# Low parts of two weight blocks in the Strassen pair jobs: a negated copy and an adding transfer in place of a VectorE subtraction

## The chip, the cores and the metric

The kernel runs on one core of one Trainium2 chip. The metric is the device time of one execution in microseconds, the median of several runs. The core has a matrix engine (PE; its weight loads are shown apart as PEld), VectorE (DVE), ScalarE (ACT), GpSimd (POOL), SyncE (SP, which here only issues transfers) and 16 DMA engines that all queues share.

## The reference

One layer of a streaming encoder, 512 tokens of width 1024, all in float32: a first SwiGLU feed-forward network (FFN) with half-step residual, a mixer (a gated recurrent branch and a windowed attention branch), and a second FFN of the same form. Each sub-layer stands between two RMS norms.

```python
def swiglu(x, w1, w3, w2):
    return (jax.nn.silu(x @ w1) * (x @ w3)) @ w2

f = swiglu(rms_norm(h, ffn1_pre_g[l]), ffn1_w1[l], ffn1_w3[l], ffn1_w2[l])   # D_FF = 2816
h = h + 0.5 * rms_norm(f, ffn1_post_g[l])
...
h = h + rms_norm(merged @ w_o[l], mix_post_g[l])
f = swiglu(rms_norm(h, ffn2_pre_g[l]), ffn2_w1[l], ffn2_w3[l], ffn2_w2[l])
return h + 0.5 * rms_norm(f, ffn2_post_g[l])
```

## The kernel before

**Numbers in two parts.** The matrix engine takes a rounded 32-bit type (`float32r`). To keep float32 accuracy every operand is held as a high part (the value rounded, written by an ACT copy) and a low part (the value minus its high part, written by a DVE subtraction). `split2` (lines 193 to 196) does the two. Every product is three: high weights by high data, low weights by high data, high weights by low data (lines 205 to 207, or 845 to 847 in the pair jobs).

**The stages.** The head loads x, transposed, and the first three weight units in quarters (lines 1000 to 1008): `load_x` brings one row block of x, `load_w(u, kp)` a quarter of weight unit u. All go out on SP's queue but the first block of x, which ACT issues. While these land, nine products on zeros warm the matrix engine (line 998); after that lines 1034 to 1048 split each quarter and multiply it. Then come the first units of FFN 1, its pair jobs, its second product (w2), the mixer, the first units of FFN 2, its pair jobs, and its w2 with the final norm.

**The pair jobs** (class `Pairs`, lines 850 to 972). The two hidden products of an FFN, x @ w1 and x @ w3, are done for two blocks of 128 hidden columns at a time, as a 2 x 2 block product with Strassen's seven products in Winograd's form. A job is one weight matrix for one pair of blocks; jobs alternate between w1 and w3. FFN 1 has 16 jobs, FFN 2 has 18. The two weight tiles `ra` and `rb` (512 KB each, 128 partitions of 4 KB) hold the blocks a11, a12 and a21, a22, 512 columns each. `prep(m, i)` prepares job m in five pieces, most of them while job m - 1 runs:

- i = 0: four block sums by DVE into the tiles S12 and S34 (lines 888 to 891).
- i = 1: high and low part of a11 and a12 together, that is of the whole tile `ra` (line 893, through `both` and `split2`).
- i = 2 and i = 3: the same for S12 and S34.
- i = 4: the same for a22; then the raw tiles and the sums are given back.

`run` (lines 904 to 972) writes a job's order by hand. Each `mm_s` is one of the seven products, 12 matmuls of 128 x 128 by 256 columns: a11 into bank bu, ACT copies bu to q1; s1 into bank bx, ACT copies bx to q5; then the previous job's last product, a22 (`last`, lines 961 to 970); then `prep(n + 1, 1)`; s2, added into bu, and ACT copies it to u; `prep(n + 1, 2)`; a12 (`c11`); s4 and DVE's sum; `prep(n + 1, 3)`; s3 and DVE's sum; Silu by ACT after a w1 job or the product of the two halves by DVE after a w3 job; `prep(n + 1, 4)`, `prep(n + 2, 0)` and the loads for job n + 3 by SP.

Within each engine this is the order of execution: nothing reorders it. Engines wait for each other by semaphores at the tiles. The first product of job n + 1 reads the high part of a11 in its first matmul and the low part in its second. In job 0 of FFN 1 there are also `late` hooks (lines 1179 to 1183): high and low parts of the data blocks b22, t3 and t4, which are first read in that job and the next.

**What sets the order around it.** Before the pair jobs, work is queued with `later(n, fn)` and run at `point()`, which `mm_feat` and `mm_s` call; the five pieces of job 0 are placed by hand (lines 1064 to 1068 and 1084 for FFN 1, 1550 for FFN 2). All tiles of 4 KB a partition come from one pool of 43 slots, in which a tile that is written waits for the last reader of the tile before it.

Of the kernel before, what the change touches and what calls it, by code (L numbers as in the profile page):

```python
# [11 lines left out]
F32R = mybir.dt.float32r  # L12
AF = mybir.ActivationFunctionType
ALU = mybir.AluOpType

P = 128
# [35 lines left out]
def hybrid_layer(ctx: ExitStack, tc: tile.TileContext, a: dict, out: bass.AP):  # L52
    nc = tc.nc
    act, dve, pool, pe, sp = nc.scalar, nc.vector, nc.gpsimd, nc.tensor, nc.sync
# [8 lines left out]
    def slot(shape, dt=F32, name="s"):  # L63
        uid[0] += 1
        return sb.tile(shape, dt, tag="slot", name=f"{name}_{uid[0]}")

    def bank(name="ps"):
        uid[0] += 1
        return pp.tile([P, 512], F32, tag="ps", name=f"{name}_{uid[0]}")
# [95 lines left out]
    def get(nm, i, ahead=2, rawahead=3):  # L165

        k = st["get"]
        assert order[k] == (nm, i), (order[k], nm, i)
        dma_to(k + 1 + ahead)
        split_to(k + 1 + ahead)  # L170
        dma_to(st["split"] + rawahead)
        st["get"] += 1
        return pairs.pop(k)
# [5 lines left out]
    def later(n, fn, rank=1):  # L179
        uid[0] += 1  # L180
        due.append((now[0] + n, rank, uid[0], fn))
# [11 lines left out]
    def split2(hi, lo, src):  # L193

        act.activation(hi, src, AF.Copy)  # L195
        dve.tensor_tensor(out=lo, in0=src, in1=f32(hi), op=ALU.subtract)  # L196
# [14 lines left out]
    def unit(nm, i, **kw):  # L211
        w = get(nm, i)
        ps = bank("f")
        mm_feat(ps, w, **kw)
        return ps
# [273 lines left out]
    def w2_gemm(nm, hid, gpost_name, scale, gpre_name, first, h_src, h_dst):  # L489
# [159 lines left out]
        for due_, cost, fn, k in reversed(plan):  # L649
            cur = min(cur, due_ - W2_LEAD) - cost / W2_FILL  # L650
            if fn:
# [184 lines left out]
    QH = 4 * P  # L836
# [13 lines left out]
    class Pairs:  # L850
# [13 lines left out]
        def prep(self, m, i):  # L864
            if m >= len(self.jobs):
                return
            k = self.k0 + 2 * m
            if i == 0:
                if k not in loaded or k + 1 not in loaded:
                    self.raws(m)  # L870
                s12, s34 = slot([P, 2 * QH], name="S12"), slot([P, 2 * QH], name="S34")
                self.w[m] = {"r": (raws.pop(k), raws.pop(k + 1)), "s": (s12, s34)}
            W = self.w[m]
            (ra, rb), (s12, s34) = W["r"], W["s"]
            a11, a12, a21, a22 = ra[:, :QH], ra[:, QH:], rb[:, :QH], rb[:, QH:]

            def both(src, w=2 * QH):
                hi = slot([P, w], F32R, name="whi")
                lo = slot([P, w], F32R, name="wlo")
                split2(hi, lo, src)  # L880
                return hi, lo

            def halves(p, a, b):
                W[a] = p[0][:, :QH], p[1][:, :QH]
                W[b] = p[0][:, QH:], p[1][:, QH:]

            if i == 0:
                dve.tensor_tensor(out=s12[:, :QH], in0=a21, in1=a22, op=ALU.add)
                dve.tensor_tensor(out=s12[:, QH:], in0=s12[:, :QH], in1=a11, op=ALU.subtract)
                dve.tensor_tensor(out=s34[:, QH:], in0=a12, in1=s12[:, QH:], op=ALU.subtract)  # L890
                dve.tensor_tensor(out=s34[:, :QH], in0=a11, in1=a21, op=ALU.subtract)
            elif i == 1:
                halves(both(ra), "a11", "a12")
            elif i == 2:
                halves(both(s12), "s1", "s2")
            elif i == 3:
                halves(both(s34), "s3", "s4")
            elif i == 4:
                t = slot([P, 2, QH], F32R, name="w22")
                split2(t[:, 0, :], t[:, 1, :], a22)  # L900
                W["a22"] = t[:, 0, :], t[:, 1, :]
                del W["r"], W["s"]

        def run(self, tail, hooks={}):
            X = self.X
            assert st["get"] == st["split"] == self.k0, (st, self.k0)
            st["get"] = st["split"] = self.k0 + 2 * len(self.jobs)
            last = lambda: None
            for n, (nm, f) in enumerate(self.jobs):
                W = self.w.pop(n)  # L910
                first = nm == self.na
                tmp = slot([P, 4, 256], name="ct")
                q1, q5, u = (tmp[:, i, :] for i in range(3))
                c = slot([P, 2, SEQ], name="cc")
                if first:
                    self.c1[f] = c
                bu, bx, bc = (bank("c")[:, :256] for _ in range(3))
                at = lambda i: [f() for f in hooks.get((n, i), ())]
                mm_s(W["a11"], X["b11"], bu)
                act.activation(q1, bu, AF.Copy)  # L920
                if n == len(self.jobs) - 1:
                    tail()
                at(1)
                mm_s(W["s1"], X["t1"], bx)
                act.activation(q5, bx, AF.Copy)
                at(2)
                last()
                self.prep(n + 1, 1)
                mm_s(W["s2"], X["t2"], bu, True)
                del W["s1"], W["s2"]  # L930
                act.activation(u, bu, AF.Copy)
                at(3)
                self.prep(n + 1, 2)

                def c11():
                    mm_s(W["a12"], X["b21"], bc)
                    del W["a11"], W["a12"]
                    dve.tensor_tensor(out=c[:, 0, :256], in0=bc, in1=q1, op=ALU.add)

                if n < len(self.jobs) - 1:  # L940
                    c11()
                mm_s(W["s4"], X["b22"], bx, True)
                dve.tensor_tensor(out=c[:, 0, 256:], in0=bx, in1=u, op=ALU.add)
                self.prep(n + 1, 3)
                mm_s(W["s3"], X["t3"], bu, True)
                del W["s3"], W["s4"]
                dve.tensor_tensor(out=c[:, 1, 256:], in0=bu, in1=q5, op=ALU.add)
                if n == len(self.jobs) - 1:
                    c11()
                if first:  # L950
                    act.activation(c[:, 0, :], c[:, 0, :], AF.Silu)
                    act.activation(c[:, 1, 256:], c[:, 1, 256:], AF.Silu)
                else:
                    c1 = self.c1[f]
                    dve.tensor_tensor(out=c1[:, 0, :], in0=c1[:, 0, :], in1=c[:, 0, :], op=ALU.mult)
                    dve.tensor_tensor(out=c1[:, 1, 256:], in0=c1[:, 1, 256:], in1=c[:, 1, 256:], op=ALU.mult)
                self.prep(n + 1, 4)
                self.prep(n + 2, 0)
                self.raws(n + 3)

                def last(W=W, bu=bu, c=c, f=f, first=first):
                    mm_s(W.pop("a22"), X["t4"], bu, True)
                    if first:
                        act.activation(c[:, 1, :256], bu, AF.Silu)
                    else:
                        c1 = self.c1.pop(f)
                        dve.tensor_tensor(out=c1[:, 1, :256], in0=bu, in1=c1[:, 1, :256], op=ALU.mult)
                        if f in self.hid.apart:
                            self.hid.c[f] = c1
                        self.hid.f += [c1[:, 0, :], c1[:, 1, :]]  # L970

            last()
# [7 lines left out]
    raw3 = [slot([P, D], name="raw_first") for _ in range(NS)]  # L980
# [4 lines left out]
    def load_x(k, q=sp):  # L985
        q.dma_start(out=xts[k // 2][:, k % 2, :], in_=a["xT"][k * P : (k + 1) * P, :])

    def load_w(u, kp):
        nm, i = order[u]
        c = slice(kp * 2 * P, (kp + 1) * 2 * P)  # L990
        sp.dma_start(out=raw3[u][:, c], in_=a[nm][i * P : (i + 1) * P, c])


    warm = slot([P, 512], F32R, name="warm")
# [3 lines left out]
        pe.matmul(psw, warm[:, :P], warm, start=True, stop=True)  # L998

    load_x(0, act)  # L1000
    sp.dma_start(out=vec, in_=a["vec"])
    for kp in range(KT // 2):
        load_w(0, kp)
        if kp:
            load_x(2 * kp)
        load_w(1, kp)
        load_w(2, kp)
        load_x(2 * kp + 1)
    dma_to(NS + 2)
# [5 lines left out]
    pairs_a = Pairs("w1a", "w3a", NC1, X1, hid)  # L1015
# [48 lines left out]
    pairs_a.prep(0, 0)  # L1064
    ps.append(unit("w3a", 1))
    pairs_a.prep(0, 1)
    p1 = unit("w1a", 2)
    pairs_a.prep(0, 2)

# [103 lines left out]
    end = 2 * 2 * (NC1 - 2)  # L1173
# [163 lines left out]
    for t in range(NT):  # L1337
        ps = bank("v")
        c = slice(t * P, (t + 1) * P)
# [207 lines left out]
        later(2 + i, lambda i=i: X2.update({f"t{i + 1}": to_slots(tn[i])}))  # L1547
    pairs_b = Pairs("w1b", "w3b", NC2, X2, hid)
    end = 2 * 2 * (NC2 - 2)
    for i, at_ in enumerate((end - 7, end - 4, end - 3, end - 2, end - 1)):  # L1550
        later(at_, lambda i=i: pairs_b.prep(0, i))
    later(end, lambda: pairs_b.prep(1, 0))
    swiglu_units("w1b", "w3b", 2, NC2, hid)
# [23 lines left out]
PRE_AT = {"xr": [("w2b", 2, 2, 2), ("w2b", 8, 8, 2)], "xg": [("w2b", 4, 7, 1)], ("wg", 13): [("w2b", 6, 1, 1)], "wao": [("w2b", 14, 4, 1)]}  # L1577
W2_LOAD = (14, 9, 8, 8)
P0A, P0B = 6, 8
W2_LEAD = 2.5  # L1580
W2_RAW = 4
W2_FLUSH = 2.5
# [57 lines left out]
```

## Time and profile before

| | us |
|---|---|
| median of 3 runs | 1120.33 (1120.18 to 1120.45) |
| profiled execution | 1120.09 |
| its span, first instruction to last | 1118.3 |
| PE busy | 1109.7 |
| PEld busy | 987.7 |
| DVE busy | 907.3 |
| ACT busy | 607.8 |
| POOL busy | 34.7 |

The span is the time from the first to the last instruction that the profile shows; the rest of an execution's time lies around it. The pair jobs run from 72.4 to 235 us (FFN 1) and from 820.5 to 1003 us (FFN 2). In a row of the timeline the first number is the start in us from the span's start, the second the duration; then engine, line, operation, tile written and tiles read, and in brackets how long the engine was idle before it and what ended the wait. A row of the waits has the engine and tile that waited, what it waited for, the sum in us, how often, and the longest. A row of the DMA issues has the transfer, the issuing queue, how often, the size and the median time from issue to landing.

### The profile page before, as it was taken

The numbers are of one execution on the slowest core, as the hardware profiler recorded it, in microseconds if no ns is written. First come the engines' busy times: TensorE is split into PE (matmuls) and PEld (weight loads), VectorE is DVE, ScalarE is ACT, GpSimd is POOL, SyncE is SP. The second block draws the span as 40 slices with busy tenths as digits, with TensorE's granted clock in tenths as the row PEclk, the third lists the DMA queues.
The fourth block names the chain that finished last, engine by engine and source line by source line (L and its number), as shares of the span: only waits on it lengthen the run. The fifth ranks groups of instructions, "written<-read, shape, count | busy, mean of one in ns | idle before, by whom it ended". The sixth has DMA issues, their size and how long they took to land.

```text
span 1118.3 us, 17215 instructions
## 1 busy us (share of the span) xinstructions
PE 1109.7 (99%) x6613; PEld 987.7 (88%) x6613; DVE 907.3 (81%) x1609; ACT 607.8 (54%) x1072; POOL 34.7 (3%) x60
## 2 busy tenths in 40 slices
PE   9999999999999999999999999999999999999997
PEld 7889999988889887888888888888999999998886
DVE  5999888888887777886799877777868888887995
ACT  7555555564455368945655664355644555555352
POOL 0000000000000000001021111000000000000000
PEclk9999999999999999999999999999999999999999
DMA  9863332260554444536232335562333322357543
GB/s 343 148 165 102 114 96 94 77 225 1 173 203 159 162 156 149 182 117 225 76 95 76 95 95 218 199 241 79 133 121 104 114 90 101 95 205 268 178 177 113
DMA packets 50482, 161.12 MB, mean 144 GB/s; under 512 B 5536, under 2 KB 7072, under 8 KB 50400
## 3 DMA queue, kind: packets, MB, share of 16 engines
q1 hardware_dynamic: 47808, 151.33, 39.3%
q0 software_dynamic: 2448, 8.43, 4.0%
q8 instruction: 52, 0.85, 0.3%
q10 hardware_dynamic: 144, 0.26, 0.1%
q14 instruction: 30, 0.25, 0.1%
HBM read 136.42 MB, written 22.54 MB: 142 GB/s over the span
## 4 chain that ended last, share of the span: by engine, by line
PE 98%; ACT 1%; DMA 1%; DVE 0%; DVEq 0%; issue 0%
PE f L205 12%; PE f L207 12%; PE f L206 12%; PE c L845 10%; PE c L847 10%; PE c L846 10%; PE acc L223 5%; PE acc L224 5%; PE acc L225 5%; PE acc L719 3%; PE acc L721 3%; PE acc L720 3%; PE pt L1446 1%; PE s L1410 1%; DMA t<-pre_w2b 1%; PE tr L294 1%
## 5 line engine op out<-in xcount | busy, mean ns | idle before, releaser
L205 PE MATMUL f<-uT,whi 128*128 128x512 f32 (+1 forms) x536 | 196.7, 367 | 0.0
L207 PE MATMUL f<-uT,whi 128*128 128x512 f32 (+1 forms) x536 | 195.2, 364 | 0.0
L206 PE MATMUL f<-uT,wlo 128*128 128x512 f32 (+1 forms) x536 | 195.1, 364 | 0.0
L205 PEld LDWEIGHTS f<-uT,whi 128*128 128x128 f32 x536 | 101.2, 189 | 16.9 <-issue 1.4
L845 PE MATMUL c<-Xh,whi 128*128 128x256 f32 x408 | 115.6, 283 | 0.1
L847 PE MATMUL c<-uT,whi 128*128 128x256 f32 x408 | 115.5, 283 | 0.0
L846 PE MATMUL c<-Xh,wlo 128*128 128x256 f32 x408 | 115.5, 283 | 0.0
L846 PE MATMUL c<-uT,wlo 128*128 128x256 f32 x408 | 115.5, 283 | 0.0
L847 PE MATMUL c<-Xl,whi 128*128 128x256 f32 x408 | 115.5, 283 | 0.0
L845 PE MATMUL c<-uT,whi 128*128 128x256 f32 x408 | 115.5, 283 | 0.0
L207 PEld LDWEIGHTS f<-uT,whi 128*128 128x128 f32 x536 | 101.1, 189 | 16.2
L206 PEld LDWEIGHTS f<-uT,wlo 128*128 128x128 f32 x536 | 101.2, 189 | 15.6
L196 DVE TENSOR_TENSOR wlo<-S,whi 128x1024 fp32r<-128x1024 f32 x68 | 82.9, 1219 | 16.4 <-ACT whi L195 16.4
L845 PEld LDWEIGHTS c<-Xh,whi 128*128 128x128 f32 x408 | 78.3, 192 | 0.3 <-ACT ct L920 0.3
L846 PEld LDWEIGHTS c<-uT,wlo 128*128 128x128 f32 x408 | 78.3, 192 | 0.0
L845 PEld LDWEIGHTS c<-uT,whi 128*128 128x128 f32 x408 | 78.3, 192 | 0.0
L846 PEld LDWEIGHTS c<-Xh,wlo 128*128 128x128 f32 x408 | 78.3, 192 | 0.0
L847 PEld LDWEIGHTS c<-uT,whi 128*128 128x128 f32 x408 | 78.3, 192 | 0.0
L847 PEld LDWEIGHTS c<-Xl,whi 128*128 128x128 f32 x408 | 78.3, 192 | 0.0
L195 ACT ACTIVATE whi<-S 128x1024 fp32r<-128x1024 f32 x68 | 68.2, 1050 | 0.0
L223 PE MATMUL acc<-whi,hT 128*128 128x512 f32 x160 | 62.5, 390 | 0.0
L224 PE MATMUL acc<-wlo,hT 128*128 128x512 f32 x160 | 62.3, 389 | 0.0
(406 smaller groups left out, 2741.6 us busy)
## 6 DMA issues: line engine op xcount, KB each, us to landing
raw_w2a<-in_w2a_dram SPq DMA_DIRECT2D x22, 512.0 KB, 4.6
raw_w1b<-in_w1b_dram SPq DMA_DIRECT2D x22, 512.0 KB, 4.5
raw_w3b<-in_w3b_dram SPq DMA_DIRECT2D x22, 512.0 KB, 4.5
raw_w3a<-in_w3a_dram SPq DMA_DIRECT2D x21, 512.0 KB, 4.2
raw_w1a<-in_w1a_dram SPq DMA_DIRECT2D x20, 512.0 KB, 4.6
raw_w2b<-in_w2b_dram SPq DMA_DIRECT2D x17, 512.0 KB, 4.1
h<-h SPq DMA_DIRECT2D x16, 512.0 KB, 3.7
raw_wg<-in_wg_dram SPq DMA_DIRECT2D x16, 512.0 KB, 3.9
```

The lines of the kernel that those rows point to most:

```text
L195: act.activation(hi, src, AF.Copy)
L196: dve.tensor_tensor(out=lo, in0=src, in1=f32(hi), op=ALU.subtract)
L205: pe.matmul(ps[:, c0:c1], wh[:, s], h_, start=k == 0, stop=False)
L206: pe.matmul(ps[:, c0:c1], wl[:, s], h_, start=False, stop=False)
L207: pe.matmul(ps[:, c0:c1], wh[:, s], l_, start=False, stop=k == KT - 1)
L223: pe.matmul(acc[n], x[:, 0, c], wh[:, s], start=first, stop=False, skip_group_check=True)
L224: pe.matmul(acc[n], x[:, 0, c], wl[:, s], start=False, stop=False, skip_group_check=True)
L225: pe.matmul(acc[n], x[:, 1, c], wh[:, s], start=False, stop=last, skip_group_check=True)
L719: pe.matmul(b, h[:, c], wh, start=start and n_ == 0, stop=False, skip_group_check=True)
L845: pe.matmul(ps, wh[:, s], xh, start=first, stop=False, skip_group_check=True)
L846: pe.matmul(ps, wl[:, s], xh, start=False, stop=False, skip_group_check=True)
L847: pe.matmul(ps, wh[:, s], xl, start=False, stop=k == 3, skip_group_check=True)
```

## The change

There are three edits.

1. In `prep`, the piece i = 1 of a pair job no longer writes the low parts of a11 and a12. It makes the two tiles and lets ACT write the high part. A new piece i = 5 makes the low part. For jobs 0 to 2 of each FFN (`m < ADD_FROM`, `ADD_FROM = 3`) it is the same DVE subtraction as before. From job 3 on ACT writes the negated value into the low tile, rounded as it is written, so that the tile holds the negated high part; then a transfer issued by POOL, with `accum_op=ALU.add`, adds the raw tile to it. The sum is the value minus its high part, as before.
2. In `run`, piece 1 of the next job moves from behind the previous job's last product to right behind the copy to q1, and piece 5 stands right behind the copy to q5. The placement of job 0's pieces gets a piece 5 at or right behind piece 1.
3. In the head, the first quarter of weight unit 1 (w3a) is issued by ACT, right behind its block of x, and no longer by SP as its third issue.

```diff
@@ prep
             elif i == 1:
-                halves(both(ra), "a11", "a12")
+                W["p"] = slot([P, 2 * QH], F32R, name="whi"), slot([P, 2 * QH], F32R, name="wlo")
+                halves(W["p"], "a11", "a12")
+                act.activation(W["p"][0], ra, AF.Copy)
+            elif i == 5:
+                hi, lo = W.pop("p")
+                if m < ADD_FROM:
+                    dve.tensor_tensor(out=lo, in0=ra, in1=f32(hi), op=ALU.subtract)
+                    return
+                act.activation(lo, ra, AF.Copy, scale=-1.0)
+                pool.dma_start(out=f32(lo), in_=ra, accum_op=ALU.add)
@@ run
                 mm_s(W["a11"], X["b11"], bu)
                 act.activation(q1, bu, AF.Copy)
+                self.prep(n + 1, 1)
                 if n == len(self.jobs) - 1:
                     tail()
                 at(1)
                 mm_s(W["s1"], X["t1"], bx)
                 act.activation(q5, bx, AF.Copy)
+                self.prep(n + 1, 5)
                 at(2)
                 last()
-                self.prep(n + 1, 1)
                 mm_s(W["s2"], X["t2"], bu, True)
@@ head
-    def load_w(u, kp):
+    def load_w(u, kp, q=sp):
         nm, i = order[u]
         c = slice(kp * 2 * P, (kp + 1) * 2 * P)
-        sp.dma_start(out=raw3[u][:, c], in_=a[nm][i * P : (i + 1) * P, c])
+        q.dma_start(out=raw3[u][:, c], in_=a[nm][i * P : (i + 1) * P, c])
...
     load_x(0, act)
+    load_w(1, 0, act)
     sp.dma_start(out=vec, in_=a["vec"])
     for kp in range(KT // 2):
         load_w(0, kp)
         if kp:
             load_x(2 * kp)
-        load_w(1, kp)
+            load_w(1, kp)
         load_w(2, kp)
         load_x(2 * kp + 1)
...
     pairs_a.prep(0, 1)
+    pairs_a.prep(0, 5)
...
-    for i, at_ in enumerate((end - 7, end - 4, end - 3, end - 2, end - 1)):
+    for i, at_ in enumerate((end - 7, end - 4, end - 3, end - 2, end - 1, end - 4)):
         later(at_, lambda i=i: pairs_b.prep(0, i))
...
+ADD_FROM = 3
```

## The prediction

> **What bounds the kernel now.** I read the page's head first, then the matrix engine's waits, then the pair jobs by windows, then one job instruction by instruction, and last the transfers.
>
> ```profile
> span 1118.3 us, 17215 instructions
> PE 1109.7 (99%) x6613; PEld 987.7 (88%) x6613; DVE 907.3 (81%) x1609; ACT 607.8 (54%) x1072; POOL 34.7 (3%) x60
> GB/s 343 148 165 102 114 96 94 77 225 1 173 203 159 162 156 149 182 117 225 76 95 76 95 95 218 199 241 79 133 121 104 114 90 101 95 205 268 178 177 113
> q1 hardware_dynamic: 47808, 151.33, 39.3%
> ...
> PEld acc L719 <- DMA t<-pre_w2b: 0.5, 1, 0.5
> PEld f L1046 <- ACT uT L1039: 0.4, 1, 0.4
> ...
> PEld c L845 <- ACT ct L920: 0.3, 1, 0.3
> PEld f L1048 <- DVE uT L1040: 0.3, 1, 0.3
> ...
> PEld f L1047 <- DVE wlo L196: 0.2, 1, 0.2
> ```
>
> PE is busy for 1109.7 of 1118.3 us. What it waits for is listed by tenths of a microsecond. The waits that this change can touch are the head's three (0.4, 0.3, 0.2) and the one on line 845 (0.3): 1.2 us together. The 0.5 on line 719 belongs to a load that the diff leaves alone.
>
> The pair jobs, by windows of one early job, its successor, and one of the second FFN:
>
> ```profile
> core 0: us, PE busy (x) PEld busy (x) DVE busy (x) ACT busy (x) POOL busy (x), PEclk, DMA share, GB/s
> 131.78:141.86 10.08, 10.08 (x86) 10.08 (x85) 9.00 (x15) 4.63 (x7) 0.00 (x0) 1.00 0.30 106
> 141.86:151.94 10.08, 10.08 (x86) 10.08 (x85) 7.91 (x12) 5.83 (x10) 0.00 (x0) 1.00 0.34 105
> 931.35:941.43 10.08, 10.08 (x87) 10.08 (x86) 8.70 (x13) 5.07 (x9) 0.00 (x0) 1.00 0.25 101
> ```
>
> A job is 84 products at 0.12 us = 10.08 us, the granted clock is 1.00, and PE has no gap. DVE (7.9 to 9.0 us) and ACT (4.6 to 5.8) lie beside it, POOL does nothing, the DMA engines are a third busy. So time taken from DVE here is worth nothing; only a wait that the change adds can count.
>
> **The pair jobs from the fourth on.** Jobs 3 to 15 of the first FFN and 3 to 17 of the second, 13 + 15 = 28, lose one DVE subtraction of 1.21 us each and gain one ACT copy and one POOL transfer of 512 KB. This is a job today, PE first, then ACT and DVE:
>
> ```profile
> 131.78 0.28 PE L845 MATMUL c<-Xh,whi 128*128 128x256 f32 x1
> 131.90 0.28 PE L846 MATMUL c<-Xh,wlo 128*128 128x256 f32 x1
> ...
> 133.48 0.38 ACT L920 ACTIVATE ct<-c 128x256 f32<-128x256 f32 x1 [3.02 <-PE c L847]
> 134.86 0.38 ACT L925 ACTIVATE ct<-c 128x256 f32<-128x256 f32 x1 [1.00 <-PE c L847]
> 135.14 1.05 ACT L195 ACTIVATE whi<-raw_w3a 128x1024 fp32r<-128x1024 f32 x1
> 137.74 0.39 ACT L931 ACTIVATE ct<-c 128x256 f32<-128x256 f32 x1 [1.55 <-PE c L847]
> ...
> 136.88 1.21 DVE L196 TENSOR_TENSOR wlo<-raw_w3a,whi 128x1024 fp32r<-128x1024 f32 x1
> ```
>
> The job starts at 131.78, the next one at 141.86; its second product (line 846) is the first to read the low part, at 131.90 + 10.08 = 141.98. Today the low part is ready at 138.1, 3.9 us early.
>
> After the change ACT runs q1 at 133.48; the next instruction starts 0.28 later (as line 195 does behind line 925), so the high copy runs 133.76 to 134.81. The copy to q5 keeps its 134.86. The negated copy then takes the place that the high copy has now, 135.14 to 136.19 (priced by that row; a scale is not expected to cost). The copy to u starts at 137.74 as before, and any Silu of the previous job's last block, due once its product ends at 136.1, waits at most 0.3 us for ACT and has until the bank is wanted again, a job later. ACT's 5.8 us becomes 6.9 of 10.08. Cost 0, covered by PE.
>
> The change adds two waits. POOL's transfer waits for the negated copy; behind it on POOL stands only the next job's transfer. PE waits for the landing and must have it by 141.98; behind that wait stands all of PE. The raw block that the transfer reads is given back only after the a22 copy at the job's end, as now, so no load of SP's is held longer. POOL starts about 0.1 us behind ACT, at 136.3 (a semaphore step shows as 0.04 us of issue in the chain further down). So the transfer has 5.7 us from issue to landing. No row shows an adding transfer. The nearest, four views of the DMA issues (the windows 559 to 566, 459 to 464, 132 to 141 and 300 to 314), with size and median us from issue to landing:
>
> ```profile
> BT<-bias_scr POOLq DMA_DIRECT2D x4, 128.0 KB, 2.5
> ...
> KS<-KS SPq DMA_DIRECT2D x2, 256.0 KB, 3.3
> ...
> raw_w3a<-in_w3a_dram SPq DMA_DIRECT2D x2, 512.0 KB, 4.1
> ...
> DMA packets 1219, 4.42 MB, mean 316 GB/s; under 512 B 139, under 2 KB 139, under 8 KB 1219
> ...
> bc_ffn_post_g<-in_ffn_post_g_dram POOLq DMA_DIRECT2D x1, 512.0 KB, 5.8
> bc_mix_pre_g<-in_mix_pre_g_dram POOLq DMA_DIRECT2D x1, 512.0 KB, 8.2
> ```
>
> A packet costs 0.393 x 16 x 1118.3 / 47808 = 0.147 us of one engine. 512 KB is 128 rows of 4 KB, 8 a DMA engine; the 128 KB of the BT row is 2. Moved once, POOL's transfer would land after 2.5 + 6 x 0.147 = 3.4 us: the low end. An addition has to read two operands. If each read costs a packet's time and the write runs beside it, it is 2.5 + 14 x 0.147 = 4.6. If the two reads and the write follow one another, 2.5 + 22 x 0.147 = 5.7. The same-size POOL row of 5.8 was measured with the engines at 316 GB/s, against 105 in the pair jobs; with one more pass (8 x 0.147 = 1.2) it makes 7.0, the high end. The 8.2 row stood behind another POOL transfer, which doesn't happen here. I take 4.6: the rows nearest in load and place (BT alone, and the SBUF-to-SBUF KS pair, two halves that make 512 KB in 3.3) lie below. The two raw loads of the job, issued at 132.5, are through by about 137.6, as the first packets of the addition start. It lands at 140.9, 1.1 us early. Cost 0; bounds 0 and 28 x (7.0 - 5.7) = +36 us.
>
> **Jobs 0 to 2 and the preparation of job 0** keep the DVE subtraction. In job 0 the orders on ACT and DVE change:
>
> ```profile
> 74.19 2.46 DVE L196 TENSOR_TENSOR uT<-xn,uT 128x1024 fp32r<-128x1024 f32 x2
> 76.86 1.22 DVE L196 TENSOR_TENSOR uT<-T,uT 128x1024 fp32r<-128x1024 f32 x1 [0.21 <-ACT uT L195]
> ...
> 79.86 0.28 PE L847 MATMUL c<-uT,whi 128*128 128x256 f32 x1
> ...
> 75.50 0.39 ACT L925 ACTIVATE ct<-c 128x256 f32<-128x256 f32 x1
> ...
> 85.28 0.28 ACT ct L920
> 85.56 0.04 issue
> ```
>
> The high copy (1.05 us) goes ahead of b22's on ACT. DVE's first row ends with b22's low part at 76.65, which becomes 77.7; the weights' low part follows (to 78.8), and only then t3's, to 79.9, two steps of 1.15. The product at 79.86 reads t3's: +0.1 us. The 0.3 us wait on line 845 is ACT's backlog of that job: PE waits for the q1 copy that ends at 85.56. ACT's total there is the same, but it no longer idles until q5 is ready at 75.50 and so is 0.1 to 0.2 us ahead. Together -0.1 at most likely; bounds -0.3 (the whole wait gone) and +0.5 (t3 late by a half instruction more).
>
> **The head.** Instructions and issues of the first 6 us:
>
> ```profile
> 0.75 0.41 ACTq L986 DMA_DIRECT2D xt<-in_xT_dram  x1
> 1.20 0.42 SPq L991 DMA_DIRECT2D raw_first<-in_w1a_dram  x1
> 1.67 0.42 SPq L991 DMA_DIRECT2D raw_first<-in_w3a_dram  x1
> 4.25 0.42 ACT L195 ACTIVATE whi<-raw_first 128x256 fp32r<-128x256 f32 x1 [1.78 <-DMA raw_first<-in_w1a_dram]
> 5.47 0.65 PE L1046 MATMUL f<-uT,whi 128*128 128x512 f32 x1
> 5.77 0.42 ACT L195 ACTIVATE whi<-raw_first 128x256 fp32r<-128x256 f32 x1 [0.50 <-DMA raw_first<-in_w3a_dram]
> ```
>
> The w3a quarter moves from SP at 1.67 to ACT at 1.16; every later issue of SP comes 0.46 us sooner, ACT's first work starts 0.4 later and still long before 4.25. PE's first product hangs on the w1a quarter, which stays at 1.20 and now shares the engines with the moved one. Gain at most 0.2 (the wait for wlo, as w3a arrives early); loss at most one quarter's transfer, 128 KB at the page's 343 GB/s of this slice, 0.4. Take +0.1. The Trainium skill, "DMA: Bandwidth & Descriptors", section "Issuing engines are not separate DMA queues", says that more issuing engines save issue time and no bandwidth. By that rule the gain is the 0.42 us of issue at most; no PE wait here hangs on it.
>
> **Sum.** Pair jobs 0, jobs 0 and 1 -0.1, head +0.1: 0. The profiled execution took 1120.09 us (span 1118.3 and 1.8 around it), 0.24 under the median 1120.33. So 1120.1 for an execution like the profiled one, and 1120.3 for the median, which I predict.
>
> **Rivals.** (1) Slower: the addition lands later than 5.7 us after its issue. For it: the 5.8 and 8.2 rows, and three passes of 0.147 use up all the slack. Against it: 105 GB/s in these stages. Each 0.1 us late costs 2.8 us, so it decides from 0.08 us late on: 1123 at 5.8, 1140 at 6.4, 1157 at 7.0. Chance 0.34. (2) POOL starts late because DVE holds the memory ports:
>
> ```profile
> 559.87 2.14 POOL L1391 DMA_DIRECT2D BT<-bias_scr  x4
> ...
> 630.08 1.98 POOL L1481 TENSOR_TENSOR OL<-o,OH 128x256 fp32r<-128x256 f32 x1 [7.53 <-ACT OH L1480]
> ```
>
> A POOL subtraction took 1.98 us here, and four issues in a row 2.14, 0.54 each, beside the same busy DVE. One DVE instruction of waiting (1.21) uses the 1.1 of slack, +0.1 a job, 1123; two cost 1.3 a job, 1157. Chance 0.05, as the issues show no stretch. The Trainium skill, "SBUF — State Buffer", section "Who interferes with whom", names a port pair shared by DVE and GpSimd and an exclusive lock, and finds tensor_tensor not stalling descriptor generation; the 0.54 agrees. (3) Faster: all four waits, 1.2 us, go: 1119.1, still within 0.2%; More than 2.2 us would need the clock or the product's pace to change. Chance 0.03 for that. (4) The head or job 0 slips by over 2 us: 0.02.
>
> **Numbers.** 0.2% is 2.2 us, about what a measurement of this kernel can tell from no change. Forecast 0.56: same 0.56, slower 0.34 + 0.05 + 0.02 = 0.41, faster 0.03. Alone, the forecast has 1119.1 to 1121.6. The range reaches into rival 1 to 6.4 us, which leaves some 0.16 above: 1118.9 to 1141.
>
> **What would show it.** Right: pair jobs still 10.08 us apart, no PE wait named for an adding transfer, its landing near 4.6 us, DVE some 34 us less busy and ACT 29 more. Wrong: PE waits on line 846 for that transfer, jobs longer by landing minus 5.7, or the first product of the head well after 5.5 us.

## The result, and the profile after

The change makes the kernel slower: 1131.49 us median (1128.94 to 1133.11, 4 runs), against 1120.37 (1120.18 to 1120.45, 4 runs) for the kernel before, measured beside it. The ratio is 1.0097, 95% interval 1.0082 to 1.0112, or +11 us. The profiled execution is the fastest of the four, 1128.94 us. Its span is 8.9 us longer than that of the profile before, so the trace can account for 8.9 of the 11.

The page's head, after (busy us and share by engine, then the queue that the page calls instruction, with packets, MB and share):

```profile
span 1127.2 us, 17338 instructions
PE 1112.0 (99%) x6613; PEld 988.3 (88%) x6613; DVE 875.5 (78%) x1581; ACT 634.3 (56%) x1100; POOL 58.9 (5%) x88
...
q8 instruction: 52, 0.85, 0.3%
```

DVE lost 32 us and ACT gained 27, as the edit says; neither engine was the bound. The matrix engine has as many products as before and a longer span. Its waits say where (engine and line waited for, us in total, times, longest):

```profile
PEld c L846 <- DMA wlo<-raw_w1a: 3.3, 2, 1.8
...
PEld c L846 <- DMA wlo<-raw_w3a: 2.3, 3, 1.1
...
PEld c L846 <- DMA wlo<-raw_w3b: 1.2, 1, 1.2
...
PEld c L846 <- DMA wlo<-raw_w1b: 0.8, 1, 0.8
```

7.6 us of waits on line 846, all for an adding transfer, and only 7 of the 28 transfers are in it. Jobs 8, 9 and 10 of the first FFN by windows (columns as in the prediction's windows). Each job holds the transfer for the next one: that of the first window is in time, that of the second is late, and the third begins with PE's wait for it:

```profile
152.96:163.04 10.08, 10.08 (x86) 10.08 (x85) 7.87 (x14) 5.58 (x8) 0.85 (x1) 1.00 0.57 158
163.04:173.12 10.08, 10.08 (x86) 10.08 (x85) 6.69 (x11) 6.78 (x11) 0.86 (x1) 1.00 0.56 148
173.00:185.00 12.00, 10.41 (x87) 10.21 (x86) 8.03 (x14) 5.57 (x8) 0.86 (x1) 1.00 0.57 139
```

The granted clock is 1.00 in all three. In the third window PE stands for 1.6 us. The timeline of the job before that stall: ACT's negated copy, POOL's issue, the raw loads that SP issues, and PE's first products of the next job (start, us, engine, line):

```profile
166.40 1.05 ACT L901 ACTIVATE wlo<-raw_w1a 128x1024 fp32r<-128x1024 f32 x1
...
167.74 0.86 POOL L902 DMA_DIRECT2D wlo<-raw_w1a  x1 [9.22 <-PE c L847]
...
165.42 2.46 SPq L142 DMA_DIRECT2D raw_w1a<-in_w1a_dram  x2
...
173.12 0.28 PE L845 MATMUL c<-Xh,whi 128*128 128x256 f32 x1
174.99 0.39 PE L846 MATMUL c<-Xh,wlo 128*128 128x256 f32 x1 [1.59 <-DMA wlo<-raw_w1a]
175.21 0.28 PE L847 MATMUL c<-Xl,whi 128*128 128x256 f32 x1
```

POOL starts 0.29 us after the copy ends (167.45). The second product could have run at 173.24, so the transfer had 5.5 us. It needed 7.2. The second of SP's two loads was issued at 167.55, 0.2 us before the addition. The DMA views of an undisturbed transfer (870.3 to 874.9) and of this one (167.5 to 175.5), each with the queue's packets, MB and share, and the issue's KB and median us to landing:

```profile
q0 software_dynamic: 144, 0.52, 57.5%
...
wlo<-raw_w3b POOLq DMA_DIRECT2D x1, 512.0 KB, 4.4
...
q0 software_dynamic: 144, 0.52, 33.5%
q1 hardware_dynamic: 236, 0.84, 30.8%
q8 instruction: 1, 0.02, 0.7%
...
raw_w1a<-in_w1a_dram SPq DMA_DIRECT2D x1, 512.0 KB, 4.9
wlo<-raw_w1a POOLq DMA_DIRECT2D x1, 512.0 KB, 7.2
raw_w3a<-in_w3a_dram SPq DMA_DIRECT2D x1, 512.0 KB, 3.7
```

Alone, the addition lands after 4.4 us; beside 0.84 MB of raw loads and one packet of the instruction queue, after 7.2. Landing minus issue of the transfers, worked out from their issue and landing times in the trace, by the job whose weights they make (the middle column is what the trace has in flight beside them):

| Transfers | beside them | landing, us |
|---|---|---|
| jobs 3, 5, 6, 8, 9, 15 (FFN 1) and 3, 5, 6, 8, 9, 11, 12, 14 (FFN 2) | nothing, or the end of a raw load | 4.4 to 4.5 |
| jobs 10, 11, 12, 13 (FFN 1) | raw loads issued up to 0.2 us earlier or 1.1 us later | 7.20, 6.19, 6.87, 6.50 |
| job 7 (FFN 1), jobs 10 and 13 (FFN 2) | a 16 KB instruction packet | 5.86, 6.26, 6.59 |
| the seven others | an instruction packet, a raw load for part of the time, or both | 4.7 to 5.4 |

The stalls in PE's record follow that list: 0.41 us (job 7), 1.75, 0.74, 1.42, 1.05 (10 to 13), 0.08, 0.81 and 1.13 (FFN 2), each with one product behind it that takes 0.10 longer: 8.2 us in all. The pair jobs of FFN 1 start 0.36 us later than before (72.79 against 72.43); with that it is 8.6 of the 8.9 us.

Why jobs 10 to 13? The raw loads wait until a slot is given back, so their place in the job moves. SP's issues in the kernel before, whose jobs 8 to 12 start 10.08 us apart at 151.94, 162.02, 172.10, 182.18 and 192.26:

```profile
153.60 1.25 SPq L142 DMA_DIRECT2D raw_w3a<-in_w3a_dram  x2
...
164.40 2.46 SPq L142 DMA_DIRECT2D raw_w1a<-in_w1a_dram  x2
...
174.32 2.63 SPq L142 DMA_DIRECT2D raw_w3a<-in_w3a_dram  x2
...
186.69 1.65 SPq L142 DMA_DIRECT2D raw_w1a<-in_w1a_dram  x2
...
196.78 1.65 SPq L142 DMA_DIRECT2D raw_w3a<-in_w3a_dram  x2
```

The first load of the pair starts 1.7, 2.4, 2.2, 4.5 and 4.5 us into the job, the second, by its own time in the trace, 2.2, 4.5, 4.5, 5.8 and 5.8. The addition is issued 4.7 us into the job. So in jobs 9 to 12, which hold the transfers for jobs 10 to 13, a load starts 0.2 us ahead of it, and in job 8 none does. This was to be seen before the change.

### The profile page after: what moved, and what is told of

Its sections match the earlier page's. It is cut to its first block, busy times and chain, and to the rows that moved or that the text cites. A ratio compares the mean times of both kernels' runs of the same rounds, so it can differ in the third digit from the quotient of the medians.

```text
span 1127.2 us, 17338 instructions
## 1 busy us (share of the span) xinstructions
PE 1112.0 (99%) x6613; PEld 988.3 (88%) x6613; DVE 875.5 (78%) x1581; ACT 634.3 (56%) x1100; POOL 58.9 (5%) x88
## 4 chain that ended last, share of the span: by engine, by line
PE 83%; issue 8%; DMA 5%; DVE 2%; ACT 1%; POOL 0%; DVEq 0%; POOLq 0%; SPq 0%; ACTq 0%
PE f L205 11%; PE f L206 11%; PE f L207 11%; PE c L846 6%; PE c L847 6%; PE c L845 6%; PE acc L223 5%; PE acc L224 5%; PE acc L225 5%; PE acc L720 3%; PE acc L719 3%; PE acc L721 3%; DMA raw_w3a<-in_w3a_dram 2%; DMA wlo<-raw_w3a 2%; PE pt L1458 1%
```

## Experiments

My theory: the transfer is quick when alone, and late only where other DMA packets lie beside it. Its main rival: the loss is spread over all additions and goes by their count, whatever their landing meets. The others are that the rest of the edits (the head's issue, the new order) cost the time, or that a single cause, such as the instruction packets, makes all late jobs. The expectations give these theories' numbers, with a letter for a name: L is mine, S the loss by count (a cost that comes with the additions wherever they land), O the rest of the edits, F the instruction packets, K a delay that one late job hands on to the next. A number of us with a plus sign is the change against the kernel before, measured beside it.

**No additions at all.** The threshold from which jobs add is put past the last job; head and order stay as changed.

```
-ADD_FROM = 3
+ADD_FROM = 99
```

> Edit to the changed kernel: ADD_FROM = 99, so all low parts are DVE subtractions again; the new places of the pieces and the head's edit stay. Theories L and S: 0.3 to 0.6 us over the kernel before (head 0.36, job 0 0.1). Rival O (the new order on ACT and DVE or the head carries the loss): 5 us or more over.

Measured: 1120.37 us against 1120.52, ratio 0.9999 (0.9991 to 1.0008). So the rest of the edits is not it: all of the loss comes with the additions. PE's first product, by the timeline:

```profile
5.45 0.50 PE L1057 MATMUL f<-uT,whi 128*128 128x512 f32 x1
```

It was at 5.47 before and is at 5.55 in the changed kernel's profile, so the early weight quarter costs nothing that can be told from one execution to another.

**Additions in FFN 1's jobs 10 to 13 alone.**

```
-                if m < ADD_FROM:
+                if not (self.na == "w1a" and 10 <= m < 14):
```

> Edit to the changed kernel: adding transfers only for jobs 10 to 13 of the first FFN, whose window holds raw loads in the kernel before too (issued 4.5 and 5.8 us after the job's start). Theory L: 4 to 6.5 us over the kernel before, 0.45 of it from the head and job 0, with each of the four landing after 6 us. Rival S: 4 x 0.3 + 0.45 = 1.7 us over. Rival K (the late transfers of these jobs are a consequence of the first one, which an instruction fetch delays in job 6): at most 1 us over.

Measured: 1127.63 us, ratio 1.0065 (1.0050 to 1.0079), +7.1. Four additions of 28 make two thirds of the loss, where a loss by count would be 1.6 us (4/28 of 11); that rival falls, and so does K, as no job before these four has an addition here. My own theory's upper bound of 6.5 was passed by 0.6 us. PE's waits in this kernel:

```profile
PEld c L846 <- DMA wlo<-raw_w1a: 3.7, 2, 2.0
...
PEld c L846 <- DMA wlo<-raw_w3a: 2.1, 2, 1.5
```

All four are late (7.07, 6.09, 7.44 and 6.63 us), 5.8 us of waits in its profiled execution, which at 1125.94 is below the median.

**Additions in the second FFN alone.**

```
-                if m < ADD_FROM:
+                if m < ADD_FROM or self.na == "w1a":
```

> Edit to the changed kernel: adding transfers in the second FFN alone (15). Theory L: its raw loads lie outside the additions' window, only instruction fetches meet them: 1 to 4 us over the kernel before, 0.45 of it from the head and job 0, with one to four late transfers, each with a 16 KB instruction packet in its window. Rival S: 15 x 0.3 + 0.45 = 5 us over.

Measured: 1122.66 us, ratio 1.0018 (1.0009 to 1.0027), +2.1. Fifteen additions cost a third of what four did. Two are waited for:

```profile
PEld c L846 <- DMA wlo<-raw_w3b: 0.6, 1, 0.6
...
PEld c L846 <- DMA wlo<-raw_w1b: 0.5, 1, 0.5
```

**The raw loads beside them taken away.** The eight loads of the last four blocks of w1 and w3 in FFN 1 are not issued; their jobs split two earlier blocks of w1 again. The expectation counts by the job that holds the transfer, so its 9 to 12 are the transfers for jobs 10 to 13. Everything else stays, all 28 additions too.

```
             nm, i = order[k]
+            if nm in ("w1a", "w3a") and i >= 18:
+                raws[k] = held[i % 2]
+                loaded.add(k)
+                return
...
+            if nm == "w1a" and i in (16, 17):
+                held.append(raws[k])
```

> Edit to the changed kernel: the eight raw loads of jobs 12 to 15 of the first FFN, which jobs 9 to 12 issue, are left out; their jobs read the tiles of w1a 16 and 17 again, so these jobs compute with other weights. All 28 additions stay. Theory L (raw loads in the window make the additions of jobs 9 to 12 late): their landings come back to 4.4 us and the loss falls to what instruction fetches leave, 1.5 to 5 us over the kernel before. Rival S (a cost of each addition): 10 to 12 us over, as the changed kernel. Rival F (instruction fetches make most of the loss): 8 us or more over.

Measured: 1122.08 us, ratio 1.0014 (1.0006 to 1.0023), +1.6. The four transfers that were late beside the loads land after 4.99, 4.43, 4.43 and 4.75 us, the first and the last of them beside an instruction packet, and none is waited for. One of them, and one of the second FFN that is still late (windows 188 to 192.6 and 916 to 922.2):

```profile
q0 software_dynamic: 144, 0.52, 57.5%
...
wlo<-raw_w1a POOLq DMA_DIRECT2D x1, 512.0 KB, 4.4
...
q0 software_dynamic: 144, 0.52, 43.1%
q8 instruction: 1, 0.02, 1.6%
...
wlo<-raw_w1b POOLq DMA_DIRECT2D x1, 512.0 KB, 6.0
```

So the raw loads are the larger cause, shown by taking them away, and the instruction packets fall as the only one. The second window has no data of another queue in it, only an instruction packet.

**The instruction packets moved.** In the pair stage the packets come about every 256 PE instructions, counting a product and its weight load as two. This kernel is the one with additions in FFN 2 alone, with 38 more products ahead of all others:

```
-WARM = 9
+WARM = 3
...
+    for _ in range(44):
+        pe.matmul(psw[:, :64], warm[:, :P], warm[:, :64], start=True, stop=True)
```

> The kernel with adding transfers in FFN 2 alone, and PE's instruction stream made 38 matmuls longer at its head: of the nine 512-wide warm-up products three stay, and 44 products of 64 columns follow. So every 16 KB block of PE's instructions after that is reached 38 matmuls sooner in the program, about 4.5 us at 0.12 us a matmul in the pair stage. In the run without this the landings of FFN 2's transfers, counted from 0, were late or nearly so in jobs 1, 4, 7, 10 and 13 (5.66, 4.85, 5.55, 5.99 and 5.11 us), where a block's packet fell 0.3 to 4.6 us after the issue, and 4.4 us in jobs 2, 5, 8 and 11. Theory (an instruction block's packet on one of the sixteen DMA engines makes the transfer late): the disturbed landings move to jobs 2, 5, 8, 11 and 14 (packets 2 to 4 us after the issue), 4.8 to 6.5 us, and jobs 1, 4, 7 and 10 land at 4.4. Total 1 to 4 us over the kernel before, and up to 1 more from the head. Rival (it is something of those jobs themselves, such as their place in the order of loads): 1, 4, 7 and 10 stay the late ones, within 0.4 us of their old landings, and 2, 5, 8 and 11 stay at 4.4.

FFN 2's landings, counted from 0 as in the expectation (the job is that number plus 3), without and with the shift; in bold those above 5.3 us:

| Transfer | 1 | 2 | 3 | 4 | 5 | 6 | 7 | 8 | 9 | 10 | 11 | 12 | 13 | 14 |
|---|---|---|---|---|---|---|---|---|---|---|---|---|---|---|
| without | **5.66** | 4.38 | 4.41 | 4.85 | 4.37 | 4.40 | **5.55** | 4.43 | 4.40 | **5.99** | 4.41 | 5.24 | 5.11 | 4.43 |
| with | 4.42 | **6.03** | 4.41 | 4.68 | **6.20** | 4.40 | 4.44 | **5.69** | 4.40 | 4.93 | **5.45** | 4.44 | 4.40 | 4.53 |

The late landings moved from 1, 7 and 10 to 2, 5, 8 and 11, as the theory had it; of these 11 had a raw load beside it too, until 3.1 us after its issue. 14 was touched but not late, at 4.53, and 4 and 10 did not come all the way back to 4.4. Transfer 5 with the shift, window 903.6 to 909.95 (the first two rows are 40 slices of 0.16 us: tenths of the 16 DMA engines' time, and GB/s):

```profile
DMA  0000000009999999797969593201010101010000
GB/s 0 0 0 0 0 0 0 0 0 258 232 181 206 206 181 232 155 232 155 284 129 310 103 310 77 26 0 26 0 26 0 26 0 26 0 26 0 0 0 0
...
q8 instruction: 1, 0.02, 1.7%
...
wlo<-raw_w1b POOLq DMA_DIRECT2D x1, 512.0 KB, 6.2
```

By the shares fifteen engines are done at slice 25; from there a single 4 KB packet starts every second slice (26 GB/s x 0.16 us = 4 KB). The packet records give no engine, but the reading is plain: the one that held the instruction packet, for 1.73 us by its record, does its share of the addition that much later, and the landing waits for it: 6.2 is 4.4 + 1.8. This sum fits where the packet starts with the addition. Packets of 0.95 us that came 2.5 and 3.0 us after the issue cost 1.3 and 1.6 us (transfer 8 with the shift, 10 without), more than they lasted; why stays open. The Trainium skill, "Runtime: NRT & Kernel Launch", section "Instruction fetch mechanics", has the instruction memory refilled in 16 KiB blocks of 256 instructions over the sequencer's own DMA queue; the packets of 16 KB and their spacing agree (15.3 us in the pair jobs before, some 128 products at 0.12 us and as many weight loads). It calls the cost of a block's crossing mostly hidden. For PE's own stream no row here speaks against that; the cost fell on another transfer.

The total missed: 1131.31 us, ratio 1.0091 (1.0074 to 1.0108), +10.9, where at most 5 was expected. That is the head, which I had mis-sized: the short products took 0.22 us apiece (25 in 5.38 us by the first row), and the first one that matters starts at 12.16 instead of 5.59. The next follows after 0.57 us and ten more at 0.43 each, up to 17.00, where without the shift the pace is 0.23 from the fourth on. The trace's first record of the granted clock, of 1.00, starts at 16.98 us here and at 5.92 without the shift.

```profile
2.92 5.38 PE L1010 MATMUL w<-warm 128*128 128x64 f32 x25
...
12.16 0.77 PE L1059 MATMUL f<-uT,whi 128*128 128x512 f32 x1
...
13.16 0.63 PE L1061 MATMUL f<-uT,whi 128*128 128x512 f32 x1
13.59 0.63 PE L1059 MATMUL f<-uT,whi 128*128 128x512 f32 x1
```

The first product is 6.6 us late, and the slow ones add 1.9: the pair jobs of FFN 1 start at 81.01 against 72.56, and FFN 2's first transfer is still 8.5 us behind (issue at 852.64 against 844.15); of the 10.9 us that leaves 2.4, near the 2.1 without the shift.

**A copy in place of the addition.** POOL's transfer copies the raw block and doesn't add.

```
-                pool.dma_start(out=f32(lo), in_=ra, accum_op=ALU.add)
+                pool.dma_start(out=f32(lo), in_=ra)
```

> Edit to the changed kernel: POOL's transfer copies the raw tile and doesn't add, so the low parts are wrong; same size, same place, same issue. Theory L: a packet takes 0.16 us and not 0.33, the undisturbed landing is 3.0 to 3.2 us after the issue and not 4.4, the disturbed ones are 1.3 us sooner too, and most are in time: 0 to 3 us over the kernel before. Rival S (the loss is in the order on ACT, POOL and PE, whatever the transfer does): 8 to 12 us over.

Measured: 1121.89 us, ratio 1.0013 (1.0004 to 1.0021), +1.4. The issues of POOL's transfers, first those of this kernel, then of the changed one:

```profile
wlo<-raw_w3b POOLq DMA_DIRECT2D x8, 512.0 KB, 2.8
...
wlo<-raw_w1a POOLq DMA_DIRECT2D x6, 512.0 KB, 4.3
```

```profile
wlo<-raw_w3b POOLq DMA_DIRECT2D x8, 512.0 KB, 4.6
...
wlo<-raw_w1a POOLq DMA_DIRECT2D x6, 512.0 KB, 5.3
```

Undisturbed, the copy lands after 2.8 us (3.0 to 3.2 was expected) and the addition after 4.4. By the packets' records one of 4 KB takes 0.159 us copied and 0.328 added, about twice, as two passes would. The copy is disturbed as well, up to 6.1 us, but it has 2.7 us to lose where the addition has 1.1. Adding is not what makes a transfer late; it takes away the reserve.

**The addition earlier.** The negated copy and the transfer go behind the first block's product, the high copy behind the second's. The issue comes 1.4 us sooner, and 6.9 us are there.

```
             elif i == 1:
...
-                act.activation(W["p"][0], ra, AF.Copy)
+                act.activation(lo, ra, AF.Copy, scale=-1.0)
+                pool.dma_start(out=f32(lo), in_=ra, accum_op=ALU.add)
             elif i == 5:
...
-                act.activation(lo, ra, AF.Copy, scale=-1.0)
-                pool.dma_start(out=f32(lo), in_=ra, accum_op=ALU.add)
+                act.activation(hi, ra, AF.Copy)
```

> Edit to the changed kernel: from job 3 on the negated copy and the adding transfer take the place behind the copy to q1, the high copy the place behind the copy to q5. POOL so issues about 1.35 us earlier, with the same instructions and the same transfers. Theory L (an addition takes 4.4 us by itself and is late only where raw loads or an instruction fetch share its DMA engines, 5.8 to 7.2 us against 5.5 to 5.7 that it has): nearly all of it lands in time, 0.5 to 1.3 us over the kernel before (head 0.36, job 0 0.1, the rest left over). Rival S (each of the 28 additions costs by itself, 8.2 / 28 = 0.3 us, through ACT, POOL or PE's read of it): 8 to 11 us over before, as the changed kernel.

Measured: 1122.60 us, ratio 1.0019 (1.0011 to 1.0028), +2.1: most of the loss is gone, where a loss by count would have stayed; but my 0.5 to 1.3 was missed. The earlier place lies inside the raw loads of more jobs: 12 of the 28 transfers land after more than 5.3 us, where the changed kernel had 8, and 11 of these 12 had a raw load beside them. The worst one (window 964.6 to 972.8):

```profile
q1 hardware_dynamic: 273, 0.99, 44.7%
...
raw_w3b<-in_w3b_dram SPq DMA_DIRECT2D x1, 512.0 KB, 8.9
wlo<-raw_w3b POOLq DMA_DIRECT2D x1, 512.0 KB, 8.1
```

It needs 8.1 us where nearly 7 are there. The 1.4 us bought time and more contention at once.

**The addition later.** The negated copy goes behind the last block of the previous job. That holds ACT back only where this block ends in ACT's Silu, in every second job: the 13 transfers for w1 jobs are issued 1.4 us later and have 4.1 us (3.8 in two), while the 15 for w3 jobs keep their 5.5.

```
-                self.prep(n + 1, 5)
                 at(2)
                 last()
+                self.prep(n + 1, 5)
```

> Edit to the changed kernel: piece 5 stands one product later, behind the previous job's last block, so POOL issues about 1.4 us later and has 4.2 to 4.3 us. Theory L: all 28 additions are late, the undisturbed by 0.1 to 0.3 us and the disturbed by 1.4 us more than now: 15 to 30 us over the kernel before, a PE wait in each job from the fourth on. Rival S (a fixed cost an addition): 8 to 12 us over.

Measured: 1140.99 us, ratio 1.0180 (1.0166 to 1.0194), +20.5, inside the expected 15 to 30, but not by 28 late transfers, as the edit moved 13. PE's waits:

```profile
PEld c L846 <- DMA wlo<-raw_w1a: 9.2, 6, 3.7
...
PEld c L846 <- DMA wlo<-raw_w1b: 5.7, 7, 1.5
PEld c L846 <- DMA wlo<-raw_w3a: 2.6, 3, 1.2
...
PEld c L846 <- DMA wlo<-raw_w3b: 0.6, 1, 0.6
```

All 13 transfers for w1 jobs are waited for, also the eight that land after 4.4 us (4.35 to 4.43), where the changed kernel waited for three of the 13. Of the 15 for w3 jobs only four are, and each of the four had a raw load or an instruction packet beside it; the other eleven land in time. Where the reserve is gone every transfer counts, and where it is left only disturbed ones do.

These 17 stalls add up to 17.3 us, with the 0.10 behind each to 19.0, but the span is 23.8 us longer than before. Most of the rest is in the clock. Behind three of the stalls, those of 1.9, 2.2 and 3.6 us, the granted clock is 0.50 for 3.41 us each. By windows, the first such stretch:

```profile
176.87:180.28 3.41, 3.39 (x16) 3.39 (x17) 2.46 (x4) 0.63 (x2) 0.00 (x0) 0.50 0.51 154
```

Products follow one another at 0.21 us in it, so 16 run where 28 would at 0.12. That is 1.5 us a stretch and 4.5 for the three.

No version here beats the kernel before; the best, without additions, is level with it.

## Why the prediction was wrong

The forecast was no change, 1120.3 us; the time is 1131.49, and it came by the first rival. That it lies inside the range is luck: the range reached there by a price that no row shows (below).

- **Failed: "Cost 0" of the pair jobs, in the step "The two raw loads of the job, issued at 132.5, are through by about 137.6".** This holds for the raw loads of the job it was read from. I took one job's place of the loads for all 28, and the loads move: they start 0.7 and 1.6 us into that job, and 4.5 and 5.8 us into jobs 11 and 12. In four jobs they lie on the addition, which lands after 6.2 to 7.2 us where 5.5 are there: +7.1 us when these alone add.
- **Left out of that step: the instruction packets.** The page of before listed 52 of them; they were in no term. In the changed kernel the transfer in the very job that the step was read from landed after 5.86 us, beside such a packet, and PE stood for 0.41. Over all kernels here a landing with one in it and no whole raw load beside it came 0.1 to 2.2 us late. Moving them moved the late jobs. With additions in the second FFN alone, both transfers that PE waited for had one. The view of before, 132 to 141, that gave the prediction its row of the raw loads has one too:

```profile
q8 instruction: 1, 0.02, 0.8%
```

- **The parts together.** 7.1 for jobs 10 to 13 and 2.1 for the second FFN make 9.2 of the 11.1 us. FFN 1's other jobs were not run alone; job 7's stall of 0.5 us in the trace is about a quarter of the rest. What adds the remaining 1.4 us was not traced; the two ratios' intervals leave room for it, and the runs point at the clock. The changed kernel's profiled execution has no stretch at 0.50 between its first and last product, a mean granted clock of 0.998 and 1128.94 us; the other three have 0.996 to 0.997 and 1131.4 to 1133.1 us. With four additions it is 0.998 to 0.999 with 1125.3 to 1126.1 us, and 0.995 to 0.997 with 1129.2 to 1131.1. One stretch, as in the kernel with the later addition, lowers such a mean by 0.0015 (half of 3.41 us in 1130). None of these slower executions left a trace, so this part is argued and not shown.
- **Weighed wrongly: "Against it: 105 GB/s in these stages".** A mean over the job doesn't say whether two transfers meet. In the windows of the changed kernel the job whose transfer lands after 4.52 us has 158 GB/s, the one whose transfer needs 7.20 has 148, and the next, with 6.19, has 139.
- **Too large by 0.2: the 5.7 us there.** POOL starts 0.29 us behind ACT, not 0.1, so it is 5.5. By itself this costs nothing: 4.4 leaves 1.1.
- **Right: the addition's own time.** 4.6 was taken by two passes of a packet, 4.4 measured, and a packet that adds takes twice a plain one (0.328 against 0.159 us). The sum's 0.147 was the mean over all packets of the page, thousands of them of 4 bytes. The high ends of 5.7 and 7.0, for three passes and for one more, were not needed; 7.2 came about by company.
- **The rival's pricing was wrong in form.** It made all 28 jobs equally late (2.8 us for each 0.1). Eight were late, by 0.08 to 1.75 us each. The time of 1131 stands for 6.1 us in all 28 by its formula, which no row shows.
- **Right in the sum, wrong in one step: jobs 0 and 1, and the head.** Job 0's product that waits for t3 starts at 80.28, behind pair jobs that start 0.36 us later in this execution, so +0.06 by itself (+0.1 was foretold). The wait for ACT's q1 copy went, but not as a gain: PE now waits as long at 84.68, for a sum by DVE that stands behind a subtraction. The kernel without additions has that wait too, and shows the sum of all this as nothing that can be told (0.9991 to 1.0008).
- **The POOL rival fell.** All 28 issues took 0.85 to 0.92 us, beside a DVE that was busy for 6.7 to 8.0 us in the windows above. The Trainium skill's sentence on descriptor generation not being stalled by tensor_tensor ("SBUF — State Buffer", "Who interferes with whom") agrees with that.

## What to carry to other kernels

When work moves from an engine to a DMA under a deadline, read the time that is there and the time that it needs, and then the place of every other transfer in every repetition of the loop: a mean bandwidth, or one iteration, hides a load whose phase drifts. In the views above a transfer split over sixteen engines lands with the slowest of them, so a single foreign packet of 16 KB is enough. The reserve here was 1.1 us; landings grew by up to 2.2 us with an instruction packet in them, and by up to 3.0 (3.7 in the swapped order) beside raw loads. Freeing an engine that was not the bound bought nothing here, while the deadline cost 11 us, some of it perhaps through the clock that falls behind a long stall.

## What the runs showed of the hardware

- An adding transfer between tiles takes 0.328 us for a 4 KB packet, a plain one 0.159; POOL's issue takes 0.85 us against 0.53, and 512 KB land after 4.4 us against 2.8.
- Instruction blocks of 16 KB come through the same DMA engines, about every 15.3 us in the pair jobs before, and one packet lasts 0.9 to 1.9 us by its record in the changed kernel.
- A late addition and a raw load slow each other: in the swapped order both took over 8 us, against 4.4 for an undisturbed addition and a median of 4.5 for the raw loads of this matrix (w3b) before.
- After each of these stalls of PE one product takes 0.10 us longer.
- A run of 64-column products at the head took 0.22 us apiece, more than the 0.12 us at which 256-column products follow one another in the pair jobs. Behind them ten products of 512 columns followed at 0.43 us each, and then all at 0.23, as elsewhere in the head. This goes with the clock: its first record in the trace, of 1.00, starts at 16.98 us, in the kernel before, with nine products of 512 columns, at 6.23, in the changed kernel's profile at 6.88. What was granted ahead of it has no record.
- A stall of PE can cost more than its length: behind three stalls of 1.9 to 3.6 us the granted clock fell to 0.50 for 3.41 us, 1.5 us of products each. A stall of 1.75 us in the changed kernel's profile was not followed by that.
